# Two pads and two rounded tiles that move every float32r operand by 32 bytes or more in SBUF

## The chip, the cores and the metric

One core of one Trainium2 chip. The metric is the device time of one execution of the program in microseconds. The program before takes 1569.77 us, the median of three runs (1568.62 to 1572.6).

## The reference, cut to what is computed

Five layers work on 256 tokens of width 1024, and a context of 256 tokens beside them: first two layers that act on x alone (even: sliding-window attention and a state-space mixer; odd: attention over the 64 best keys by an index), then a joint attention layer, in which x attends to itself and to the context, a gated feed-forward layer for each of the two, a state-space layer with a convolution and chunked decays over both, and a last feed-forward layer and norm for x. Nearly all the arithmetic is dense products with weights from DRAM:

```python
z = hn @ w_in                          # 1024 x 2304, 1024 x 3144, later 1536 and 6208 columns
h = h + concat([att, ssm]) @ w_out
out = (silu(a @ w_gate) * (a @ w_up)) @ w_down      # 1024 x 2816 and back, for x twice, for the context once
```

All values are float32, and the result must be close to a float32 product.

## The kernel before, in words

A product of activations and weights is made of three products in float32r, a format of four bytes that TensorE takes at one column a cycle and that keeps fewer bits than float32. Weights and activations are each split into a high part h and a low part l = value - h; what is added up in PSUM is h x h, h x l and l x h.

Weights pass through `Weights`: `fetch` brings a chunk of 128 x 1024 float32 (512 KB) into a tile raw, on SyncE's DMA queue; `load` lets ScalarE round it into a tile h (line 178) and VectorE (or GpSimd) subtract into a tile l (line 179). `wx` holds three raw, two h and two l for x, `wc` two of each for the context, and both stand in pools on the right side of SBUF. Activations stand on the left, in pairs such as nhx and nlx (normalized x, 8 blocks of 128 x 256), fh and fl (the feed-forward's hidden values) or ysH and ysL.

Two helpers use a chunk. `feat_tiles` takes 128 weight columns as the stationary operand and streams 256 tokens past them: 8 blocks times 3 products, 24 products of 256 columns. `tok_step` takes 128 tokens as the stationary operand and streams weight columns: 2 blocks, 2 halves of tokens and 3 products, 12 products of 512 columns, or 24 of 256 columns where the chunk is cut for 256. All go through `mm` (line 129). Every product comes with its own load of 128 stationary columns (LDWEIGHTS, on the engine row PEld), which runs beside the product before it. In the state-space layer's convolution (`project`) the three channel blocks are made for x and for the context with one chunk: 24 more products for each of 3 blocks in 8 groups.

Products in plain float32 are the state-space and attention ones (`pv`, `py`, `pada`, `poff`); transposes are products with ident or flip, slices of the tile misc, as the moving operand. A few masks are added as bf16 products.

SBUF is handed out in stacks, each tile a multiple of 32 bytes in its partition. On the left lie 1,024 bytes for DMA descriptors and 128 bytes of built-in constants, then the pool con, whose first tile is misc (548 float32 values, 2,192 bytes, rounded up to 2,208), then res, act, wk and the pools of the layers. So misc starts at byte 1,152, a multiple of 64, and the tiles behind it at 32 past one. On the right the stack of wx begins 32 bytes under the end of SBUF, and its tiles start at 32 past a multiple of 64 too, as those of wc and cx below it do. Within a tile the slices go in steps of 256, 512 or 1,024 bytes. Small tiles of 32 bytes stand in some pools (sink in evat, hb in ev).

The order on each engine is made by a planner with a model of the engines' times; the pools with `reuse_waits="tile"` make it wait where two tiles share bytes.

Of the kernel before, what the change touches and what calls it, by code (L numbers as in the profile page):

```python
# [8 lines left out]
F32 = mybir.dt.float32  # L9
# [79 lines left out]
def build(tc, A):  # L89
    nc = tc.nc  # L90
    T, V, S, G, SY = nc.tensor, nc.vector, nc.scalar, nc.gpsimd, nc.sync
    es = ExitStack()
    PS = bass.MemoryType.PSUM

    def D(name):
        return A[name]

    def dram(a, off, ap):
        return bass.AP(tensor=a.tensor, offset=a.offset + off, ap=ap)

    def pool(name, bufs=1, space=None, right=False):
        kw = {"side": "right"} if right else {}
        if space is not None:
            kw["space"] = space
        else:
            kw["reuse_waits"] = "tile"
        return tc.tile_pool(name=name, bufs=bufs, **kw)

    con = es.enter_context(pool("con"))
    res = es.enter_context(pool("res"))  # L110
    act = es.enter_context(pool("act"))
    wk = es.enter_context(pool("wk", 2))
# [72 lines left out]
        return [(lambda t: t, dram(a, k0 * 128 * ncols + n0, [[ncols, 128], [128 * ncols, kt], [1, 128]]))]  # L185

    cst = ExitStack()
    wx = Weights("x", *WX, SY, es)
    wc = Weights("c", *WC, SY, cst)
    cx = cst.enter_context(pool("cx", right=True))  # L190
# [230 lines left out]
    def even_layer(hook):  # L421
        with ExitStack() as st:
            p = st.enter_context(pool("ev"))
# [11 lines left out]
            at = st.enter_context(pool("evat"))  # L435
# [10 lines left out]
            pr = s0.tile([32, 128], F32, name="ar_rows")  # L446
# [134 lines left out]
            sl = ssm.enter_context(pool("ssl"))  # L581
            yH = act.tile([128, 8, 256], F32R, tag="hx", name="yH")
            yL = act.tile([128, 8, 256], F32R, tag="lx", name="yL")
            sink = at.tile([128, 8], F32, name="sink")
            SY.dma_start(sink, dram(D("ev_sinks"), 0, [[0, 128], [1, 8]]))

            def attention(m):
# [100 lines left out]
            for q in range(4):  # L688
                split(glH[:, q], glL[:, q], uT[:, q])
            glu_w = D("ev_glu_w")  # L690
            hb = p.tile([128, 4], F32, name="hb")
            V.tensor_scalar(hb, glu_b[:, 4:8], 0.5, None, op0=ALU.mult)
            for c in range(4):
                pg = psx.tile([128, 2, 256], F32, tag="d", name="pglu")
# [803 lines left out]
    def low(f, by):  # L1498
# [6 lines left out]
        (ctx_start, ctx_qkv, ctx_attend, ctx_ffn, ctx_mod1, ctx_steps), LOW))  # L1505
    hooks = {0: [c_start], 1: [c_qkv, c_attend]}
    sc_b = even_layer(lambda i: [f() for f in hooks[i]])
    odd_layer(sc_b)
    c_ffn()
# [33 lines left out]
```

## Time and profile before

| what | us |
|---|---|
| median of 3 runs | 1569.77 |
| lowest and highest | 1568.62, 1572.6 |
| the profiled execution, its time | 1569.01 |
| the profiled execution, its span | 1567.2 |
| TensorE busy in it | 1479.1 |
| VectorE busy | 1110.6 |
| ScalarE busy | 771.3 |
| GpSimd busy | 304.2 |

The span goes from the first to the last instruction of the profiled execution; its time is a little longer. A busy TensorE is one that has a product in its pipe: products overlap, so a busy time near the span says that something is always in flight, and not how fast it goes. The pace is read from the starts of products that follow each other.

### The profile page before, as it was taken

What the parts mean: (1) busy time and instruction counts of PE and PEld (TensorE: products, weight loads), DVE (VectorE), ACT (ScalarE), POOL (GpSimd) and SP (SyncE); (2) the same over time, 40 slices, a digit from 0 to 9 for tenths busy, and PEclk for the clock granted to TensorE, in tenths of its full rate; (3) what the DMA queues carried; (4) which work ended last, traced back from release to release, by engine and by line L of the source; (5) the groups of instructions that cost most, each with busy time, mean ns of one, the idle gap of its engine ahead of it and who ended that gap; (6) DMA issues with size and microseconds to landing.
All of it is one profiled execution on the core that took longest, in us unless ns stands there. A gap on an engine that the chain in (4) does not pass through costs nothing. (4 is left out here: it accounts for less than half of the span.)

```text
span 1567.2 us, 26910 instructions
## 1 busy us (share of the span) xinstructions
PE 1479.1 (94%) x10532; PEld 1263.1 (81%) x10532; DVE 1110.6 (71%) x1825; ACT 771.3 (49%) x1386; POOL 304.2 (19%) x247
## 2 busy tenths in 40 slices
PE   6799998999999999999989999889899999799998
PEld 5574555786898888687779999888789998699997
DVE  6779996667766778666556665478988876665665
ACT  4433446654545455576444444445455544454444
POOL 2415660000100100000000000238966400200000
PEclk9899999999999999999999999898999999999999
DMA  8784565566665767633666465454534433455664
GB/s 252 237 224 143 185 172 164 142 190 211 192 187 169 219 204 201 224 109 101 199 209 190 161 186 181 126 135 123 128 106 129 109 97 121 156 164 187 194 188 135
DMA packets 306174, 264.56 MB, mean 169 GB/s; under 512 B 27441, under 2 KB 260703, under 8 KB 306048
## 3 DMA queue, kind: packets, MB, share of 16 engines
q1 hardware_dynamic: 306048, 262.85, 56.2%
q8 instruction: 83, 1.36, 0.4%
q14 instruction: 43, 0.35, 0.1%
HBM read 261.47 MB, written 1.34 MB: 168 GB/s over the span
## 5 line engine op out<-in xcount | busy, mean ns | idle before, releaser
L179 DVE TENSOR_TENSOR l<-raw,h 128x1024 fp32r<-128x1024 f32 (+2 forms) x366 | 453.4, 1241 | 268.0 <-ACT h L178 237.6
L178 ACT ACTIVATE h<-raw 128x1024 fp32r<-128x1024 f32 (+2 forms) x374 | 389.0, 1042 | 411.2 <-PE pdx L129 103.9
L129 PE MATMUL pffnx<-nhx,h 128*128 128x256 f32 x704 | 170.4, 282 | 0.0
L129 PE MATMUL pffnx<-nlx,h 128*128 128x256 f32 x704 | 170.1, 282 | 0.2 <-DVE nlx L349 0.2
L129 PEld LDWEIGHTS pffnx<-nhx,h 128*128 128x128 f32 x704 | 134.3, 191 | 1.6 <-issue 1.6
L129 PEld LDWEIGHTS pffnx<-nlx,h 128*128 128x128 f32 x704 | 133.9, 190 | 1.5 <-issue 0.8
L307 POOL TENSOR_TENSOR sums<-sums,nhalf 128x1 f32<-128x1 f32 x20 | 13.0, 652 | 536.3 <-DVE sums L303 523.4
L129 PE MATMUL pffnx<-nhx,l 128*128 128x256 f32 x704 | 96.8, 280 | 0.0
L129 PE MATMUL pffnc<-nhc,h 128*128 128x256 f32 x352 | 88.9, 287 | 0.4 <-ACT nhc L348 0.4
L129 PEld LDWEIGHTS pffnx<-nhx,l 128*128 128x128 f32 x704 | 88.4, 189 | 0.4 <-issue 0.4
L129 PE MATMUL pffnc<-nlc,h 128*128 128x256 f32 x352 | 87.9, 285 | 0.1
L179 POOL TENSOR_TENSOR l<-raw,h 128x1024 fp32r<-128x1024 f32 (+1 forms) x8 | 18.5, 2312 | 353.8 <-PE pdx L129 200.5
L129 PE MATMUL pdx<-h,nhx 128*128 128x256 f32 (+1 forms) x256 | 84.8, 347 | 1.4 <-DVE cv L1284 1.3
L129 PE MATMUL pdx<-h,nlx 128*128 128x256 f32 (+1 forms) x256 | 83.0, 341 | 0.0
L894 PE MATMUL pada<-araw,cT 128*32 128x256 f32 x704 | 72.7, 401 | 10.7 <-DMA araw<-ada_w 9.8
L129 PE MATMUL pcvx<-nhx,h 128*128 128x256 f32 x256 | 73.8, 298 | 3.8 <-DVE cv L1284 3.8
L129 PE MATMUL pdx<-h,fh 128*128 128x256 f32 (+1 forms) x264 | 77.2, 318 | 0.0
L129 PE MATMUL pdx<-h,fl 128*128 128x256 f32 (+1 forms) x264 | 77.1, 317 | 0.0
L129 PE MATMUL pcvx<-nlx,h 128*128 128x256 f32 x256 | 71.8, 290 | 0.0
L129 PEld LDWEIGHTS pffnc<-nhc,h 128*128 128x128 f32 x352 | 66.5, 189 | 2.9 <-ACT nhc L348 1.0
L129 PEld LDWEIGHTS pffnc<-nlc,h 128*128 128x128 f32 x352 | 66.6, 189 | 2.1 <-DVE nlc L349 0.5
L129 PE MATMUL pdx<-l,nhx 128*128 128x256 f32 (+1 forms) x256 | 58.5, 344 | 1.4 <-DVE l L179 1.3
(620 smaller groups left out, 3875.9 us busy)
## 6 DMA issues: line engine op xcount, KB each, us to landing
araw<-ada_w SPq DMA_DIRECT2D x88, 512.0 KB
raw<-ffn_w_gate SPq DMA_DIRECT2D x66, 512.0 KB
raw<-ffn_w_up SPq DMA_DIRECT2D x66, 512.0 KB
raw<-ffn_w_down SPq DMA_DIRECT2D x54, 512.0 KB
raw<-ssm_w_in SPq DMA_DIRECT2D x48, 512.0 KB
raw<-od_w_in SPq DMA_DIRECT2D x25, 512.0 KB
raw<-attn_w_qkv SPq DMA_DIRECT2D x24, 512.0 KB
raw<-attn_w_o SPq DMA_DIRECT2D x32, 256.0 KB
```

The source lines that it names most:

```text
L129: i = T.matmul(out, l, r, start=start, stop=stop)
L178: S.activation(h[:, :n], raw[:, :n], AF.Copy)
L179: (G if self.on_pool > 0 else V).tensor_tensor(l[:, :n], raw[:, :n], h[:, :n].bitcast(F32), op=ALU.subtract)
L307: G.tensor_tensor(s[:, 3:4], s[:, j - 1:j], nhalf[:, 0:1], op=ALU.pow)
L894: T.matmul(pt[32 * q:32 * q + 32, 0:256], cT[:, k, :], raw[:, q * 256:(q + 1) * 256], start=k == 0, stop=k == 7, tile_position=(0, 32 * q))
```

## The change

A tile of 32 bytes is put ahead of misc in con, which nothing reads or writes, and another in a pool of its own at the right end of SBUF, ahead of wx. So everything in con and in the left pools moves up by 32 bytes, and the weight pools on the right move down by 32. The tiles sink and hb are allocated with 64 bytes in place of 32, and used as before through a slice, so that the tiles behind them (Tt, and glH and glL in its place) lie at a multiple of 64 too. misc itself moves from 1,152 to 1,184. No instruction is added, removed or given another shape.

```diff
--- before.py
+++ after.py
@@ -107,6 +107,7 @@
         return tc.tile_pool(name=name, bufs=bufs, **kw)
 
     con = es.enter_context(pool("con"))
+    con.tile([128, 8], F32, name="pad")
     res = es.enter_context(pool("res"))
     act = es.enter_context(pool("act"))
     wk = es.enter_context(pool("wk", 2))
@@ -185,6 +186,7 @@
         return [(lambda t: t, dram(a, k0 * 128 * ncols + n0, [[ncols, 128], [128 * ncols, kt], [1, 128]]))]
 
     cst = ExitStack()
+    es.enter_context(pool("pr", right=True)).tile([128, 8], F32, name="padr")
     wx = Weights("x", *WX, SY, es)
     wc = Weights("c", *WC, SY, cst)
     cx = cst.enter_context(pool("cx", right=True))
@@ -581,7 +583,7 @@
             sl = ssm.enter_context(pool("ssl"))
             yH = act.tile([128, 8, 256], F32R, tag="hx", name="yH")
             yL = act.tile([128, 8, 256], F32R, tag="lx", name="yL")
-            sink = at.tile([128, 8], F32, name="sink")
+            sink = at.tile([128, 16], F32, name="sink")[:, 0:8]
             SY.dma_start(sink, dram(D("ev_sinks"), 0, [[0, 128], [1, 8]]))
 
             def attention(m):
@@ -688,7 +690,7 @@
             for q in range(4):
                 split(glH[:, q], glL[:, q], uT[:, q])
             glu_w = D("ev_glu_w")
-            hb = p.tile([128, 4], F32, name="hb")
+            hb = p.tile([128, 16], F32, name="hb")[:, 0:4]
             V.tensor_scalar(hb, glu_b[:, 4:8], 0.5, None, op0=ALU.mult)
             for c in range(4):
                 pg = psx.tile([128, 2, 256], F32, tag="d", name="pglu")
```

## Rows read from the trace of the kernel before

**Rows 1.** Page: span, TensorE's busy time and instructions, ScalarE's weight chunks.

```profile
span 1567.2 us, 26910 instructions
PE 1479.1 (94%) x10532; PEld 1263.1 (81%) x10532; DVE 1110.6 (71%) x1825; ACT 771.3 (49%) x1386; POOL 304.2 (19%) x247
...
L178 ACT ACTIVATE h<-raw 128x1024 fp32r<-128x1024 f32 (+2 forms) x374 | 389.0, 1042 | 411.2 <-PE pdx L129 103.9
```

**Rows 2.** Chain that ended last, two pieces (start us, us, what, count).

```profile
1375.12 61.22 PE pffnx L129 x527
...
1466.41 62.19 PE pffnx L129 x528
```

**Rows 3.** Windows: length, PE, PEld, DVE, ACT, POOL busy (count), clock, DMA, GB/s.

```profile
1378.10:1436.10 58.00, 58.00 (x514) 58.00 (x514) 36.61 (x51) 28.63 (x42) 0.00 (x0) 1.00 0.64 191
1436.20:1451.30 15.10, 15.10 (x69) 12.39 (x68) 7.70 (x9) 6.10 (x9) 0.00 (x0) 1.00 0.53 181
1466.20:1528.40 62.20, 62.20 (x530) 62.20 (x530) 38.99 (x55) 29.64 (x43) 0.00 (x0) 1.00 0.64 189
1528.40:1543.80 15.40, 15.40 (x68) 12.52 (x67) 7.69 (x9) 6.07 (x9) 0.00 (x0) 1.00 0.53 179
```

**Rows 4.** Same view, a stretch at the low clock, and its timeline of PE.

```profile
1008.28:1011.46 3.18, 3.18 (x16) 3.18 (x16) 2.10 (x4) 1.52 (x4) 0.00 (x0) 0.50 0.00 0
...
1009.00 0.42 PE L129 MATMUL pcvx<-nlx,h 128*128 128x256 f32 x1
...
1011.35 0.41 PE L129 MATMUL pcvx<-nlx,h 128*128 128x256 f32 x1
```

**Rows 5.** Timeline of PE (start us, us, what): a bf16 product and the next.

```profile
440.90 0.27 PE L129 MATMUL plo<-sel,flip_b 128*128 128x256 bf16 x1
441.01 0.60 PE L129 MATMUL plo<-KTo,QTo 128*128 128x256 f32 x2
```

**Rows 6.** Timeline of PE: two plain float32 products, with one between them.

```profile
121.05 0.38 PE L129 MATMUL py<-m,CT 128*32 128x256 f32 x1
...
121.48 0.38 PE L129 MATMUL py<-m,CT 128*32 128x256 f32 x1
```

**Rows 7.** Windows of line 178 alone: ScalarE's copies, one for each weight chunk.

```profile
0.00:300.00 300.00, 45.39 (x43) 0.95 0.64 191
300.00:790.00 490.00, 136.71 (x132) 1.00 0.60 182
790.00:995.00 205.00, 68.29 (x66) 0.98 0.60 186
995.00:1162.00 167.00, 25.86 (x25) 0.93 0.47 123
1162.00:1370.00 208.00, 44.42 (x43) 0.98 0.40 119
1370.00:1567.00 197.00, 68.34 (x66) 0.98 0.57 175
```

**Rows 8.** Windows of all engines by stage: PE, PEld, DVE, ACT, POOL, clock, DMA.

```profile
0.00:300.00 300.00, 264.21 (x1600) 174.27 (x1601) 233.49 (x408) 139.34 (x310) 109.25 (x99) 0.95 0.64 191
300.00:790.00 490.00, 485.95 (x3472) 405.14 (x3471) 335.04 (x587) 265.37 (x472) 17.18 (x21) 1.00 0.60 182
790.00:995.00 205.00, 200.30 (x1576) 187.55 (x1576) 131.81 (x207) 95.05 (x145) 2.14 (x4) 0.98 0.60 186
995.00:1162.00 167.00, 143.03 (x1059) 134.32 (x1058) 128.10 (x184) 80.18 (x138) 116.71 (x78) 0.93 0.47 123
1162.00:1370.00 208.00, 197.48 (x1368) 180.47 (x1368) 158.85 (x264) 101.71 (x190) 57.59 (x44) 0.98 0.40 119
1370.00:1567.00 197.00, 188.12 (x1466) 181.39 (x1466) 123.31 (x179) 89.67 (x132) 1.37 (x2) 0.98 0.57 175
```

**Rows 9.** Groups by line: transposes by ident (L1111) and by flip (L841).

```profile
L1111 PE MATMUL ptcx<-misc,P 128*128 128x128 f32 x128 | 20.1, 277 | 0.0
...
L841 PE MATMUL ppt<-misc,Tt 128*128 128x128 f32 x24 | 4.4, 279 | 0.0
```

## The prediction

> **What bounds the kernel now.** Read first the page's busy times. TensorE (PE) is busy for 1479.1 us of the 1567.2 us span [rows 1]. Busy PE is not PE at its peak, so the second view is the chain of work that ended last: its last pieces are long unbroken runs of float32r products, 527 and 528 in a row in the last feed-forward stage, with no wait between them [rows 2]. There the time is count times pace, so the third view is the pace of such a run: a stretch of the windows view divided by the products that start in it. One should take some 106.7 ns for 256 columns at the granted 2.4 GHz (PEclk 1.00). In the first half of that stage 512 products take 58.0 us, 113.3 ns each; in the second half 528 take 62.2 us, 117.8 ns each; products of 512 columns take 15.1 us for 66 (228.8 ns) and 15.4 us for 66 (233.3 ns) [rows 3]; a row counts up to three neighbours that reach over its edge. So every float32r product is 6 to 10% slower than its columns, and nothing it waits for explains that.
>
> Three rows narrow down where the loss comes from. At the lower clock it is gone: 11 products from 1009.00 to 1011.35 us take 213.6 ns each, which is 256 columns at 1.2 GHz [rows 4]. A bf16 product of 256 columns hands over after 0.11 us [rows 5], and a plain float32 one, which streams each column twice, after 0.215 us, which is 512 columns at 2.4 GHz [rows 6]; the operands of both lie at 32 bytes past a multiple of 64, as the float32r ones do now. So the loss shows only where four bytes per column are wanted at every cycle of the full clock: it is in the supply from SBUF, not in the array or in the issue.
>
> The size fits straddling. A 256-column operand is 1 KB. Starting at 32 past a multiple of 64 it touches 17 blocks of 64 bytes where an aligned one touches 16; a block is 16 columns, 17 blocks are 272 cycles, and 272 cycles at 2.4 GHz are 113.3 ns, the faster pace to the last digit [rows 3]. It doesn't fit everything: 512 columns would touch 33 blocks, 220 ns, and the rows say 228.8 and more; and the same operands at the same addresses run at 113.3 and at 117.8 ns in the two halves, so at least 4.4 ns depend on something else.
>
> **The change, part by part.** No instruction is added or removed. Four allocations grow. Today the constants begin with misc (2192 bytes, rounded up to 2208), so everything behind it on the left lies 32 past a multiple of 64; the tiles of wx and wc on the right do too. After it, all 8212 float32r products have both operands at a multiple of 64. The trace of before has no float32r product that does, so the worth is bounded, not read.
>
> Number: the 374 weight chunks [rows 1] each serve 24 products of 256 columns, or 12 of 512 (two units each); the context's share in the convolution adds 8 x 3 x 8 x 3 = 576. Together 374 x 24 + 576 = 9552 units. Pace now: the mean of 113.3, 117.8, 228.8/2 and 233.3/2 [rows 3] is 115.6 ns. Pace after, best end: 109 ns, what a stream without loss shows (0.11 us in [rows 5], half of 0.215 us in [rows 6]). Worst end: 117.8 ns, the slower pace everywhere. I take the best end, because the loss has the size of one block per product and vanishes in each row where a 17th block would be hidden. Saving: 9552 x 6.6 ns = 63 us of PE work, 0.158 us a chunk.
>
> How much of that reaches the end is read stage by stage, from the chunks per stage [rows 7] and the other engines there [rows 8]. The shares are my estimates from those rows:
> - 0 to 300 us: 43 chunks, 6.8 us. DVE is busy 233 of 300 us, POOL 109, and the state-space scan orders the work: a third, 2.3.
> - 300 to 790: 132 chunks, 20.9 us; PE busy 486 of 490: 85%, 17.7. The rest is in attention, where PE waits its turn behind DVE and ACT.
> - 790 to 995: 66 chunks, 10.4 us; PE 200 of 205: 95%, 9.9.
> - 995 to 1162: 25 chunks, 4.0 us; POOL 117 of 167 us, PE only 143: 40%, 1.6.
> - 1162 to 1370: 43 chunks and the 576 products (in part before), 10.6 us; PE 197 of 208, but groups wait for decays and gates: 70%, 7.4.
> - 1370 to 1567: 66 chunks, 10.4 us; nothing but PE: 95%, 9.9.
>
> The sum is 48.8 us. What is late next: the weight chunk's split on DVE and its copy on ACT (DVE 123 of 197 us in the last stage) and the DMAs (0.57 of the 16 engines) both have room for a pace 6% faster [rows 8]. The profiled execution took 1569.0 us, 0.8 under the median of 1569.8 and 1.8 over its span, so 1569 - 49 = 1520 us.
>
> Ident and flip move too: misc goes from a multiple of 64 to 32 past one, flip from 16 past to 48 past. Transposes by ident take 277 ns, by flip 279 [rows 9], so the start of that operand costs at most 2 ns on the program's 541 transposes by ident, 1 us, and I take nothing. Weight loads from DRAM land 32 bytes further down, DVE and ACT read and write there: no row has the other alignment; DMA has 43% of its engines free in the last stage and DVE 37%, so either sign is covered there, and I allow 3 us both ways elsewhere. The larger sink and hb push the tiles behind them by 32 to 64 bytes, and where pools of different times share space a wait can appear or go: 0 to 3 us, taken as nothing.
>
> [...]
>
> **The rivals.** A, *alignment is nothing to the stream*: the extra sixteenth is the rate at which SBUF feeds four-byte columns, wherever they start. For it: the loss doubles with the columns, as a rate would, and a block counted per product would not; and the two paces at one address. Against it: only that 113.3 ns is 272 cycles to the digit. It gives 1570 us.
> B, *half of it*: straddling is the part that varies, and all settles at 113.3 ns, or a like part goes. 9552 x 2.3 ns = 22 us, times the same survival (49/63), 17 us: 1552 us.
> C, *slower*: today moving and stationary operand start 64 bytes apart within 128 bytes (activations 32, weights 96); the left moves up by 32 and the right down by 32, so afterwards both start at 64. If the weight load and the stream, which run side by side (PEld busy 181 of 197 us in the last stage [rows 8]), get in each other's way when they start in the same half, the slower pace holds everywhere: 9552 x 2.2 ns x 0.78 = 16 us, 1586 us. It decides against the change when more than the share of products now at 117.8 goes there and nothing is won on the straddle. The two paces at equal addresses say that such a meeting of streams exists.
> D, *it doesn't do what it says*: a consumer is left at 32. Tile sizes are multiples of 32, and those ahead of float32r tiles that are odd multiples come in pairs, but for the ones that the diff changes; so small, and like A in time.
>
> **How the numbers follow.** Forecast 0.45 (1520 us, own range 1503 to 1536: all 63 us survive, or half), B 0.17, A with D 0.22, C 0.16. What a measurement of this kernel can tell from no change is about 0.3%, 5 us. B lies beyond that bound, so faster is 0.62; A and a little of C give 0.23 for the same; slower is 0.15. The range goes from 1503 to 1582: it takes in the forecast's own range, B and A, and the smaller half of C.
>
> **What would show it.** In the last stage, the 512 and 528 products without a wait: right at 109 to 110 ns, B at 113, A at both paces as now, C at 118 throughout; products of 512 columns at 216, 227, 229 to 233, or 233 and more. The weight load's pace follows. The stages before 300 and from 995 to 1162 us should shrink least. Transposes by ident at 277 ns, as before. It would be wrong if the paces don't move (the step "the loss has the size of a block" falls), or if they do and the span doesn't: then the survival shares are wrong, and the wait that took the place is to be found on DVE's l, ACT's h or raw's DMA.

## The result and the profile after

The changed kernel takes 1585.78 us, the median of four runs (1581.62 to 1587.9); the kernel before, on the same chip, takes 1569.19 (1567.05 to 1572.6). The ratio is 1.010, its 95% interval 1.0073 to 1.0128: slower by one per cent. The forecast was 1520 us and its range ended at 1582; rival C, which had it slower, gave 1586.

First the page of after: the span, the engines, and the group of ScalarE's weight copies that answers to the one in [rows 1].

```profile
span 1584.2 us, 26910 instructions
PE 1502.0 (95%) x10532; PEld 1286.8 (81%) x10532; DVE 1111.9 (70%) x1825; ACT 772.0 (49%) x1386; POOL 302.5 (19%) x247
...
L179 ACT ACTIVATE h<-raw 128x1024 fp32r<-128x1024 f32 (+2 forms) x374 | 388.6, 1041 | 426.1 <-PE pdx L130 106.2
```

The instruction counts are those of before, and so is the order on every engine. TensorE is busy 22.9 us longer. A copy of a weight chunk takes 1041 ns (1042 before), all of VectorE 1111.9 us (1110.6): the other engines did not notice their new addresses. Transposes by ident and flip, the groups of [rows 9], didn't either:

```profile
L1113 PE MATMUL ptcx<-misc,P 128*128 128x128 f32 x128 | 20.0, 277 | 0.0
...
L843 PE MATMUL ppt<-misc,Tt 128*128 128x128 f32 x24 | 4.5, 279 | 0.0
```

So the time went into the pace of the products. The windows of the last feed-forward stage, as in [rows 3] (length, PE, PEld, DVE, ACT, POOL busy with counts, clock, DMA share, GB/s):

```profile
1390.10:1451.40 61.30, 61.30 (x514) 61.30 (x513) 36.60 (x51) 28.74 (x42) 0.00 (x0) 1.00 0.61 182
1451.40:1466.40 15.00, 15.00 (x69) 12.40 (x68) 7.67 (x9) 6.07 (x9) 0.00 (x0) 1.00 0.52 181
1466.50:1545.60 79.10, 79.10 (x662) 79.10 (x661) 50.30 (x71) 35.39 (x49) 0.00 (x0) 1.00 0.63 185
1545.60:1560.60 15.00, 15.00 (x69) 12.41 (x68) 7.70 (x9) 6.07 (x9) 0.00 (x0) 1.00 0.56 183
```

Each count holds three neighbours from over the edge. 511 products of 256 columns in 61.30 us are 120.0 ns each, and 659 in 79.10 us again 120.0; before it was 113.3 in the first half and 117.8 in the second. Products of 512 columns take 15.00 us for 66, 227.3 ns, in both halves; before 228.8 and 233.3. So the two kinds moved in opposite directions. A cycle here is an estimate, the time of one column at the full clock: 256 columns took 213.6 ns at a granted clock of 0.50 [rows 4], so 106.8 at 1.00, 2.4 columns a ns; and m1 below has 106.7 ns between products of 256 and 512 columns (120.0 and 226.7). In such cycles 120.0 ns are 288, 32 more than the columns; the 512-wide ones, taken from the starts of a long run, need 545, 33 more. For these two widths the loss no longer grows with the columns: it is 32 cycles or so for each product.

The growth by stage, in windows whose bounds lie at the same products as those of [rows 8]:

```profile
0.00:305.03 305.03, 269.07 (x1600) 177.98 (x1601) 234.02 (x408) 139.49 (x310) 108.24 (x99) 0.95 0.63 188
305.03:798.66 493.63, 490.90 (x3472) 410.59 (x3471) 335.55 (x587) 265.93 (x472) 17.24 (x21) 1.00 0.60 181
798.66:1006.14 207.48, 203.56 (x1576) 191.20 (x1576) 131.82 (x207) 94.96 (x145) 2.05 (x3) 0.98 0.61 184
1006.14:1173.45 167.31, 145.47 (x1058) 136.85 (x1058) 126.24 (x184) 80.31 (x138) 116.01 (x78) 0.93 0.46 122
1173.45:1381.80 208.35, 199.73 (x1368) 183.36 (x1368) 160.91 (x264) 101.60 (x189) 57.62 (x44) 0.98 0.40 119
1381.80:1584.00 202.20, 193.23 (x1466) 186.78 (x1466) 123.34 (x179) 89.66 (x132) 1.37 (x2) 0.97 0.56 170
```

The stages are 5.0, 3.6, 2.5, 0.3, 0.4 and 5.2 us longer, together 17.0. Since the order is the same, each product has its twin in the other trace. Summed over those that nothing holds up in either trace, the pace of 256-wide products cost 1.1, 5.5, 3.8, 2.6, 3.2 and 5.7 us in the six stages, 22.0 in all, and that of 512-wide ones gave back 1.5. So 20.5 us of pace became 17.0 us of span.

### The profile page after: what moved, and what is told of

It reads as the page before. It is cut to its first block, busy times and chain, and to the rows that moved or that the text cites. A ratio compares the mean times of both kernels' runs of the same rounds, so it can differ in the third digit from the quotient of the medians.

```text
span 1584.2 us, 26910 instructions
## 1 busy us (share of the span) xinstructions
PE 1502.0 (95%) x10532; PEld 1286.8 (81%) x10532; DVE 1111.9 (70%) x1825; ACT 772.0 (49%) x1386; POOL 302.5 (19%) x247
## 5 line engine op out<-in xcount | busy, mean ns | idle before, releaser
L179 ACT ACTIVATE h<-raw 128x1024 fp32r<-128x1024 f32 (+2 forms) x374 | 388.6, 1041 | 426.1 <-PE pdx L130 106.2
L130 PE MATMUL pffnx<-nhx,h 128*128 128x256 f32 x704 | 174.7, 285 | 0.0
L130 PE MATMUL pffnx<-nlx,h 128*128 128x256 f32 x704 | 174.4, 285 | 0.3 <-DVE nlx L351 0.2
```

The source lines that it names most:

```text
L130: i = T.matmul(out, l, r, start=start, stop=stop)
L179: S.activation(h[:, :n], raw[:, :n], AF.Copy)
```

## What was to be told apart

Call distance the start of a product's weights less the start of its moving operand, in bytes. Modulo 128 it is 64 before (32 and 96) and 0 after (64 and 64), but for some 500 of the 8,212 products, which kept 64; m1 shows that modulo 256 is the right measure. Theory 1: the load of the next weights and the stream get in each other's way, and the distance alone sets the pace; where the operands lie matters to nothing. Theory 2: the pace comes from the absolute starts, so that a start at a multiple of 64 is what costs. The bench kernels m1 to m3 below are trains of products on one pair of tiles, with x as filling: they compute nothing of the reference, and serve for the pace alone.

## m1: one pair of tiles, the starts varied

```diff
+ mo = m0 // 4 + (i % 7) * n
+ wo = w0 // 4 + (i // 2 % 8) * 128
+ T.matmul(pt[0:w, 0:n], wt[:, wo:wo + w], mv[:, mo:mo + n], start=i == 0, stop=i == count - 1)
```

> A bench of its own: 38 runs of 96 float32r products (48 of 512 columns) without a wait between them, which compute nothing of the reference; only the byte at which the streamed operand starts (m) and the distance d to the start of the weights are varied. Theory 1 (the stream of one product and the weight load of the next meet in SBUF; only the distance between them counts): at d = 0 a product of 256 columns takes 120 ns, at d = 64 it takes 113 or 118 ns, the same for m = 0, 32, 64 and 96; the loss comes from the weight load, so with 512 columns it stays at some 14 ns (227 ns), with 64 weight columns it is half (113 ns) and with 32 a quarter (110 ns). Theory 2 (the start itself counts): 120 ns for m = 0 and 64 whatever d is, 113 or 118 ns for m = 32 and 96. Theory 3 (neither; the pace comes from how a run happens to begin): paces between 113 and 120 ns without an order in d or m, and the repeats of d = 64 and d = 0 at the end differ among themselves.

The timeline of PE (start, length, tile, count); the pace of a group is the time from its start to the next group's start, divided by its count. Groups pad to paf have the moving operand at 0 and the weights at 48, 64 and 80; pai and paj have the weights at 128 and 160; par and pas have the two at 32 and 96, and at 64 and 64; paw to pay are 512-wide at distances 0, 32, 64, and pbb at 192; pbi to pbl alternate 64, 0, 64, 0.

```profile
46.12 11.47 PE L45 MATMUL pad<-mv,wt 128*128 128x256 f32 x96
57.43 11.05 PE L45 MATMUL pae<-mv,wt 128*128 128x256 f32 x96
68.31 11.57 PE L45 MATMUL paf<-mv,wt 128*128 128x256 f32 x96
...
102.62 11.55 PE L45 MATMUL pai<-mv,wt 128*128 128x256 f32 x96
114.01 11.68 PE L45 MATMUL paj<-mv,wt 128*128 128x256 f32 x96
...
204.76 11.47 PE L45 MATMUL par<-mv,wt 128*128 128x256 f32 x96
216.07 11.67 PE L45 MATMUL pas<-mv,wt 128*128 128x256 f32 x96
227.58 11.47 PE L45 MATMUL pat<-mv,wt 128*128 128x256 f32 x96
...
261.70 11.09 PE L45 MATMUL paw<-mv,wt 128*128 128x512 f32 x48
272.63 11.35 PE L45 MATMUL pax<-mv,wt 128*128 128x512 f32 x48
283.82 11.36 PE L45 MATMUL pay<-mv,wt 128*128 128x512 f32 x48
295.02 11.40 PE L45 MATMUL paz<-mv,wt 128*128 128x512 f32 x48
...
317.42 11.16 PE L45 MATMUL pbb<-mv,wt 128*128 128x512 f32 x48
328.41 11.06 PE L45 MATMUL pbc<-mv,wt 128*128 128x512 f32 x48
...
394.04 11.04 PE L45 MATMUL pbi<-mv,wt 128*128 128x256 f32 x96
404.92 11.68 PE L45 MATMUL pbj<-mv,wt 128*128 128x256 f32 x96
416.44 11.47 PE L45 MATMUL pbk<-mv,wt 128*128 128x256 f32 x96
427.75 11.68 PE L45 MATMUL pbl<-mv,wt 128*128 128x256 f32 x96
```

pae, at distance 64, takes 10.88 us for 96, 113.3 ns; pad and paf beside it take 117.8 and 118.8. pas, both operands at 64, takes 11.51 us, 119.9; par, both at the starts of the kernel before, 117.8. Over the last 48 products of each group, distance 0 gave 120.0 ns with the moving operand at 0, 32, 64 and 96 alike, and distance 64 gave 113.3 or 117.8. The other distances under 128 gave 118.3 at 16 and 32, 117.8 at 48, 118.8 at 80, 118.6 at 96 and 120.0 at 112. 512-wide it is the other way round: 226.7 ns at distance 0 in the second half of its group (227.7 over the whole) and 233.3 at 32 and 64. All paces of both kernels appear here, with no other engine at work. Theory 2 falls. Theory 1 holds in its main point: the distance decides which paces occur, and the place of the operands doesn't. That the distance alone sets the pace does not hold, since the repeats of 64 differ among themselves, as theory 3 had it.

Modulo 128 turned out to be too coarse. At 128 the pace is 118.6 ns (pai) where 0 and 256 have 120.0, at 160 it is 120.0 where 32 has 118.3, and 512-wide it is 229.0 at 192 (pbb) where 64 and 320 have 233.3. At 256 and 384 the 256-wide paces are those of 0 and 128 again. So the distance counts modulo 256. Taken so, the kernel before has mainly two: 64 where activations stream past weights, and 192 where activations are the weights. Its 512-wide runs in [rows 3] stand at 192, and m3, further down, saw both of their paces there: about 229 ns behind most trains, 233.3 behind two.

Two things did not fit. pbi and pbk have the same addresses, and run at 113.3 and 117.8: the one comes after products with 32 weight columns, the other after products at distance 0. So the two paces of [rows 3] are no matter of stage or neighbours; a train keeps what it begins with. And with only 64 or 32 weight columns the pace was 113.3 at distance 0 as at 64 (pbe to pbh): a loss of 16 cycles stays, though the weight columns shrink to a quarter; theory 1 had 110 for 32 columns.

## e1 and e2: distance against alignment in the kernel

e1 is the kernel before with 64 bytes ahead of misc: nothing lies at a multiple of 64, and the distance is 0. e2 is the changed kernel with 64 more: everything lies at a multiple of 64, and the distance is 64 modulo 128 (modulo 256, the 64 and the 192 of the kernel before have changed places).

```diff
 # e1, against before
+    con.tile([128, 16], F32, name="pad")
 # e2, against after
-    con.tile([128, 8], F32, name="pad")
+    con.tile([128, 24], F32, name="pad")
```

> The kernel before with 64 bytes ahead of the constants and nothing else: everything stays 32 past a multiple of 64, but the left side's operands now start at 96 within 128 bytes, as the weights on the right do (distance 0). Theory 1 (the distance counts): 120 ns for 256 columns, 227 ns for 512, and 1586 us, like the changed kernel, though nothing is aligned to 64. Theory 2 (the alignment counts): 113 and 118 ns as before, 1570 us.

> The changed kernel with a pad of 96 bytes in place of 32 ahead of the constants: all operands at a multiple of 64 as in the changed kernel, but the left ones at 0 and the weights on the right at 64 within 128 bytes (distance 64, as in the kernel before). Theory 1 (the distance counts): 113 and 118 ns as before, 1570 us. Theory 2 (the alignment counts): 120 ns and 1586 us.

e1 took 1586.3 us (ratio 1.0096, 1.0074 to 1.0118), as the changed kernel; e2 took 1572.05 (1.0006, 0.9995 to 1.0018), as the kernel before. The windows of the last stage, e1 first: two runs of 256-wide products and one of 512-wide.

```profile
1391.00:1452.00 61.00, 61.00 (x510) 61.00 (x509) 36.63 (x51) 28.33 (x42) 0.00 (x0) 1.00 0.61 180
1467.10:1546.20 79.10, 79.10 (x662) 79.10 (x661) 50.24 (x71) 35.40 (x49) 0.00 (x0) 1.00 0.64 186
1452.00:1467.00 15.00, 15.00 (x69) 12.40 (x68) 7.67 (x9) 6.07 (x9) 0.00 (x0) 1.00 0.54 180
```

Then e2, the same three:

```profile
1380.70:1441.10 60.40, 60.40 (x514) 60.40 (x514) 36.63 (x51) 28.59 (x42) 0.00 (x0) 1.00 0.61 184
1456.80:1531.50 74.70, 74.70 (x662) 74.70 (x661) 50.15 (x71) 35.34 (x49) 0.00 (x0) 1.00 0.68 197
1441.30:1456.70 15.40, 15.40 (x69) 12.40 (x68) 7.76 (x9) 6.09 (x9) 0.00 (x0) 1.00 0.56 178
```

e1 runs at 120.0 ns (659 in 79.10 us) and 227.3 (66 in 15.00). e2 has both paces of before, with the halves exchanged: 117.7 in the first (513 in 60.40 us), 113.4 in the second (659 in 74.70), and 233.3 for 512 columns. Alignment to 64 bytes buys nothing and costs nothing that these runs resolve (e2's interval ends at 0.18%, some 3 us); the distance accounts for the 16 us. The changed kernel's own trace says it too: 237 products of 256 columns that kept distance 64 in it, on tiles that moved together, average 116.9 ns, against 119.75 for the 6,027 at distance 0.

The 113.3 and 120.0 ns of m1 (pbi and pbj), at distances that differ by the weights' address alone, say that the address of the load changes the stream's pace. By what path it does so, no run shows.

## e3 and e4: half of the change

Only the left pad, or only the right one: the distance becomes 32 either way, with other absolute starts.

```diff
 # e3, against before
+    con.tile([128, 8], F32, name="pad")
 # e4, against before
+    es.enter_context(pool("pr", right=True)).tile([128, 8], F32, name="padr")
```

> The change's first edit alone: 32 bytes ahead of the constants, nothing on the right, no tile rounded up. The left operands lie at a multiple of 64, the weights on the right stay 32 past one; the distance in the products with streamed activations goes from 64 to 32. Theory 1 (distance, priced by the first bench: 118.3 ns at 32 against 113.3 or 117.8 at 64): about half to three quarters of the change's loss, 1576 to 1584 us. Theory 2 (alignment of the left side): the whole loss in the products that stream activations.

> The change's second edit alone: 32 bytes at the right end, nothing on the left, no tile rounded up. The weights lie at a multiple of 64, the activations don't; the distance is 32 as with the left pad alone. Theory 1 (distance): the same as the left pad alone, 1576 to 1584 us. Theory 2 (alignment): another time than the left pad alone, as different operands are aligned.

e3 took 1580.04 us (1.0073, 1.005 to 1.0096), e4 1580.48 (1.007, 1.0043 to 1.0097). One window of each, first e3:

```profile
1387.40:1447.90 60.50, 60.50 (x513) 60.50 (x511) 36.59 (x51) 28.49 (x42) 0.00 (x0) 1.00 0.61 183
```

and e4:

```profile
1387.00:1447.50 60.50, 60.50 (x513) 60.50 (x513) 36.60 (x51) 28.61 (x42) 0.00 (x0) 1.00 0.61 184
```

511 products in 60.50 us are 118.4 ns in both; over all products of the kind the means are 118.32 and 118.31, the bench's 118.33 at distance 32. Two layouts with different absolute starts and one distance are the same kernel in time.

## m2: how the loss depends on width, and what makes the two paces

The same bench with 128 to 512 columns on 32 or 128 weight columns; then distances 48 to 80 in steps of 4, each after a group at distance 0; then narrow products (32 weight columns) ahead of trains. One such sequence (columns, weight columns, the two starts, count):

```diff
+ ("s", 256, 128, 0, 0, 96), ("s", 256, 32, 0, 64, 1), ("s", 256, 128, 0, 64, 96)
```

> A second bench in the manner of the first, computing nothing of the reference: the streamed width with 32 and 128 weight columns, fine steps of the distance d, and what stands ahead of a run. Theory 1a (the loss has two parts: a sixteenth of the columns which the stream loses by itself, and the meeting with the weight load): with 32 weight columns the pace is N x 17/16 at 2.4 GHz for every width N (128: 56.7, 192: 85, 384: 170, 512: 227 ns), and at d = 0 with 128 weight columns 16 cycles more at 256 columns. Theory 1b (a fixed 16 cycles each product): N + 16 cycles (128: 60, 512: 220 ns). Of the two paces at d = 64: theory S (the pace is set by how the run begins and then holds) expects 117.8 ns behind a run at d = 0 and 113.3 ns behind a run with 32 weight columns, and that one product with 32 weight columns in between is enough to turn it; theory R (it is random) expects no such order.

With 32 weight columns, products of 128 columns took some 144 cycles, 16 over, as 1b had it (60 ns, an estimate: 56 of them took 3.70 us from 13.00 us on, the eight before 107.5 ns each, and seven more at that pace leave 60 ns for the rest). Those of 192, 256, 320, 384, 448 and 512 columns took 88.4, 113.5, 143.3, 173.3, 202.2 and 231.6 ns, or 212, 272, 344, 416, 485 and 556 cycles: 20, 16, 24, 32, 37 and 44 over their columns. That is neither a sixteenth of the columns nor a fixed 16, so both readings of the rest (1a and 1b) fall, and what it is stays open. With 128 weight columns at distance 0 it was 32 over at 256, 320, 384 and 512 columns, but 76 at 192 (111.4 ns) and 48 at 448 (206.4 ns). At distance 64 products of 192, 320 and 384 columns took just as long as at 0 (111.4, 146.9 and 173.3 ns), and those of 448 took 37 over (202.3 ns). So the distance counts at 256, 448 and 512 columns and not at the three other widths; and at 384 columns 32 weight columns are no quicker than 128. The meeting of load and stream is thus no general price of distance 0, and what makes it depend on the width is open.

The entry is clearer. Timeline of PE: pay at distance 64 after a group at 0; and pbp at 0, one narrow product, pbr at 64.

```profile
260.18 11.47 PE L54 MATMUL pay<-mv,wt 128*128 128x256 f32 x96
271.49 11.68 PE L54 MATMUL paz<-mv,wt 128*128 128x256 f32 x96
...
449.63 11.68 PE L54 MATMUL pbp<-mv,wt 128*128 128x256 f32 x96
461.15 0.28 PE L54 MATMUL pbq<-mv,wt 128*32 128x256 f32 x1
461.27 11.04 PE L54 MATMUL pbr<-mv,wt 128*128 128x256 f32 x96
472.15 11.68 PE L54 MATMUL pbs<-mv,wt 128*128 128x256 f32 x96
```

pay takes 11.31 us, 117.8 ns a product. One product with 32 weight columns ahead of it, and the same train (pbr) takes 10.88 us, 113.3, as theory S had it. In the three benches together 64 ran at 117.8 in all six trains behind distance 0, and at 113.3 in all six behind narrow products; at 320, which is 64 modulo 256, the one train behind distance 0 (m1's pan) ran at 113.5. Among the distances from 48 to 80 only 52 and 76 ran at 113.3 behind a group at distance 0.

## m3: the entry at more distances

Each distance is entered three times: after distance 0, after 512-wide products at 192, and after four narrow products.

```diff
+ ("s", 256, 128, 0, 0, 48), ("s", 256, 128, 0, d, 72), ("s", 512, 128, 0, 192, 24),
+ ("s", 256, 128, 0, d, 72), ("s", 256, 32, 0, d, 4), ("s", 256, 128, 0, d, 72)
```

> A third bench in the same manner, computing nothing of the reference: each distance d is entered behind a run at d = 0, behind products of 512 columns, and behind four products with 32 weight columns. In the second bench d = 52 and 76 went to 113.3 ns behind a run at d = 0, where 64 went to 117.8. Theory S1 (the fast pace of 113.3 ns exists at most distances, and how a run begins decides; 52 and 76 have the better entry): 113.3 ns in all three entries at 52 and 76, 117.8 then 113.3 behind the narrow products at 64 and 192. Theory S2 (luck of that entry): 52 and 76 come out at 113.3 in some of the entries only.

The timeline of PE for distance 52 (pai, pak and pam are the trains, paj the 512-wide entry, pal the narrow one):

```profile
60.49 8.37 PE L51 MATMUL pai<-mv,wt 128*128 128x256 f32 x72
68.70 5.66 PE L51 MATMUL paj<-mv,wt 128*128 128x512 f32 x24
74.19 8.80 PE L51 MATMUL pak<-mv,wt 128*128 128x256 f32 x72
82.83 0.63 PE L51 MATMUL pal<-mv,wt 128*32 128x256 f32 x4
83.30 8.33 PE L51 MATMUL pam<-mv,wt 128*128 128x256 f32 x72
```

At 52 the train runs at 114.0, 120.0 and 113.3 ns (8.21, 8.64 and 8.16 us for 72) by what came ahead of it. At 64 the three are 117.8, 117.8 and 113.3; at 204 they are 123.1, 113.3 and 113.3. Only 76 and 192 gave 113.3 from all three. At 44, 60, 68, 84, 180 and 212 no entry changed the pace, which was between 117.2 and 120.0. So S1 is right for 76 and S2 for 52, and neither as a whole: 113.3 appeared at only five of the fourteen distances. 120.0 isn't the worst pace there is, and 113.3 remains the best.

## e5 and e6: entries and 512-wide products in the kernel

e5 puts twelve narrow products ahead of the feed-forward's and other long trains; each writes a part of PSUM that the train then starts anew. e6 adds 192 bytes ahead of ysH, so that the 192 products of 512 columns of the state-space output go from distance 64 to 0.

```diff
 # e5, against before (in feat_tiles; tok_step likewise)
+        if lead:
+            mm(uses[0][1][0:32], wh[:, 0, 0:32], uses[0][0](0)[0], True, True, mark)
 # e6, against e5
+            p.tile([128, 48], F32, name="pady")
```

> The kernel before, with 12 products of 256 columns and 32 weight columns put ahead of long runs (each half of x's two feed-forward layers, their way back where it turns to 256 columns, and the odd layer's gates); their results are overwritten by the next product, so the output is the same. Theory S (the entry sets the pace until something interrupts): the runs behind them take 113.3 ns; some 2,000 of the products that now take 117.8 ns are behind one, 2,000 x 4.4 ns = 9 us less 12 x 0.11 us, 1561 to 1566 us. Theory R (random, or fixed by the distance): both paces as before, 1570 to 1572 us.

> The same with 192 bytes ahead of ysH and ysL, which serve 192 products of 512 columns as weights: their distance to the streamed operand goes from 64 to 0 (within 256 bytes). Theory 1 (the distance counts, and with 512 columns 0 is the best, 226.7 against 233.3 ns in the benches): these products take 226.7 ns in place of 231 to 236 and the time is 192 x 6.7 ns = 1.3 us under the kernel with the lead products alone. Against: 512 columns take 231 to 236 ns wherever ysH starts.

e5 took 1584.56 us (1.0101, 1.0081 to 1.0121), well outside what was expected. Two windows of its last stage, both behind a lead:

```profile
1392.70:1450.90 58.20, 58.20 (x515) 58.20 (x515) 36.62 (x51) 28.63 (x42) 0.00 (x0) 1.00 0.64 191
1466.30:1544.00 77.70, 77.70 (x662) 77.69 (x661) 50.14 (x71) 35.19 (x49) 0.00 (x0) 1.00 0.65 189
```

The first runs at 113.4 ns (513), the second at 117.7 (660): in the kernel one narrow product ahead of a train did not always settle its pace. Once it did: in the odd layer's gates the 72 products ahead of the lead at 441.82 us take 8.48 us, 117.8 ns each, and the 70 behind it 7.94 us, 113.4 each, at the same distance. And the planner, given twelve more products, put all engines into another order from TensorE's 290th product on; the last stage begins at 1392.7 us instead of 1378.1, with the paces of before in it. So e5 shows that the leads did not steer reliably, and not what steering would be worth.

e6 took 1582.98 us (1.0084, 1.0059 to 1.0108), 1.6 under e5, with intervals that overlap. The 512-wide run it was made for:

```profile
1361.50:1375.60 14.10, 14.10 (x63) 11.65 (x62) 8.94 (x11) 7.49 (x12) 2.04 (x1) 1.00 0.65 201
```

62 products in 14.10 us are 227.4 ns, where the same run in e5 and in the kernel before has 233.5. The pace followed the distance as in the bench. Over all 192 the mean goes from 233.3 to 228.4, so they could save 192 x 5 ns, about 1 us, and that is less than these runs resolve.

## e7 and e8: the two distances that the bench liked

Both start the activations elsewhere in a widened tile, so that 256-wide products stand at distance 76 (e7) or 192 (e8, modulo 256; 64 modulo 128), and keep the pad of e6 ahead of ysH. The order on the engines is that of before.

```diff
+    def act_tile(tag, name):
+        return act.tile([128, 2112], F32R, tag=tag, name=name)[:, 61:2109].rearrange("p (k t) -> p k t", k=8)
 # e8: [:, 32:2080]
-          H = act.tile([128, 8, 256], F32R, tag="h" + key, name="nh" + key)
+          H = act_tile("h" + key, "nh" + key)
```

> The kernel before with the activations' tiles widened by 256 bytes and used from byte 244 on, and 192 bytes ahead of ysH; no instruction and no order changes. The 5184 products that stream activations past weights go from a distance of 64 to 76, 1296 products with those activations as weights from 192 to 180, the 192 with ysH from 64 to 0. Theory S1 (at 76 a run finds the fast pace from any beginning, as in all four entries of the benches): 113.3 ns for the first kind (now 116.1 in the mean), 118.2 and 233.3 ns for the second (now 116.3 and 231.2), 227 ns for ysH: -14.5 + 2.9 - 1.2 us of PE work, at the share of 0.78 some 10 us: 1556 to 1564 us. Theory S2 (in the kernel the beginnings are too many): the paces stay mixed, 1566 to 1575 us.

> The same with the activations used from byte 128 on: the 5184 products at a distance of 192, the 1296 at 64, ysH at 0. At 192 the benches found 113.3 ns in four entries and 117.8 in one. Theory S1: as at 76, 1556 to 1566 us, if the kernel's beginnings are like the four. Theory S2: 113.3 and 117.8 ns mixed as before, 1566 to 1575 us. If the pace at 192 is 117.8 throughout: 1575 to 1580 us.

e7 took 1584.33 us (1.0109, 1.0088 to 1.013). Two windows of its last stage:

```profile
1400.00:1454.00 54.00, 54.00 (x440) 54.00 (x439) 31.98 (x46) 24.54 (x37) 0.00 (x0) 1.00 0.59 177
1486.00:1548.00 62.00, 62.00 (x519) 62.00 (x518) 38.17 (x53) 28.32 (x43) 0.00 (x0) 1.00 0.63 187
```

Some 517 products in 62.0 us, 120 ns; in the first half of that stage it was about 123 (some 438 products in 54.0 us), and over all 4,727 at that distance the mean is 120.63. The bench's 113.3 did not carry over, and both theories missed. In the bench the streamed operand stood at 0 and the weights at 76, in e7 they stand at 20 and 96 modulo 128; whether that is what matters was not separated.

e8 took 1573.24 us (1.0042, 1.0024 to 1.006). Both halves of its last stage:

```profile
1379.60:1440.10 60.50, 60.50 (x515) 60.50 (x515) 36.64 (x51) 28.69 (x42) 0.00 (x0) 1.00 0.61 184
1471.30:1533.00 61.70, 61.70 (x527) 61.70 (x526) 38.48 (x54) 29.14 (x43) 0.00 (x0) 1.00 0.64 189
```

514 products in 60.50 us and 524 in 61.70: 117.7 ns in both. Here nearly every train took the slower of the two paces (mean 117.40 over 4,862), where the kernel before has both (mean 116.09), and the quicker ysH products didn't make up for it. The time lies in S2's range, but the paces were hardly mixed; 117.8 throughout had been given 1575 to 1580. e2 has these two distances as well, and half of its last stage ran at 113.4: the distance says which paces there are, and not which of them a train gets. No version found beats the kernel before.

## Why the prediction was wrong, step by step

- *What bounds the kernel.* Right: long trains of float32r products, whose time is count times pace. The pace moved, and the last stage, which has nothing else, moved by the full price: 5.7 less 0.5 us of pace, 5.2 us of span.
- *"The loss is in the supply from SBUF, not in the array or in the issue."* Right for the part that moved. It didn't ask which of the two supplies: with 128 weight columns the loss at 256 columns goes from 16 to 32 cycles, 113.3 to 120.0 ns, by the weights' address alone (m1), so the load of the next weights belongs to it. For the 16 cycles that stay at every distance no run shows where they arise.
- *"The size fits straddling", one block of 64 bytes per product.* This is the step that failed. That 272 cycles are 17 blocks of 16 columns was a coincidence of numbers: at distance 0 the pace is 288 cycles with the operand aligned to 64 (pas) or not, and 272 appears aligned (e2's second half) and not aligned (before). What the runs show in its place is the distance between weights and stream: with every operand aligned the 256-wide pace is 120.0 at distance 0 (the changed kernel) and 117.7 and 113.4 in e2. The two misfits that the prediction itself named, 512 columns at 228.8 ns instead of 220 and two paces at one address, were the evidence against it.
- *The pace after.* I took the best end, 109 ns, borrowed from bf16 and plain float32 [rows 5, 6]. Neither row is the pace of a product in a stream: the kernel issues 64 py products and the trace has 128 records of them, so 0.215 us is half a product, and the bf16 product at 442.53 us hands over after 0.03 us, not 0.11. At a granted clock of 1.00 no train of 48 or more float32r products of 256 columns showed a pace under 113.3, in the kernels or in the benches. The worst end, 117.8, was too good by 2.2 ns: at distance 0 it is 120.0. An end taken from the worst of two rows is not a bound on a layout that none of them has.
- *Rival C.* What it named is what happened: weights and stream that start together, and a slower pace. Its mechanism, the two getting in each other's way, is borne out for 256 columns by the narrow weights, whose products take 113.3 ns at distance 0 as at 64 (m1); it does not cover the 512-wide products, which got quicker there, nor the widths that don't care (m2). Its price was wrong: it moved all products to 117.8 ns, 2.2 ns on 9,552 units, 21 us. Measured, the 256-wide ones went from 116.1 to 119.6 ns in the mean and the 512-wide ones got quicker by 1.3; by twin products 22.0 less 1.5 us, 20.5. Two errors of price cancel, and 1586 agrees with 1585.8 in part by luck. A chance of 0.16 was too low, since the two paces at equal addresses, which I counted for it, had no other explanation in the rows.
- *Survival.* 0.78 of the pace was to reach the end; the span grew by 17.0 us on 20.5 of pace, 0.83, which looks like a hit and is luck in part. In the first stage 3.9 us of the growth are not pace; without them 13.1 of 20.5 us came through, 0.64. 790 to 995 (2.5 of 3.4 us) and 300 to 790 (3.6 of 5.2) came out under their 95% and 85%. From 995 to 1370 us, where I had 40 and 70%, 0.7 of 5.6 us survived: waits took up most of the rest, as TensorE's idle time in these two stages fell from 34.5 to 30.5 us. The first stage grew by 5.0, of which pace is 1.1. Some 2.4 us of that come in one place, where TensorE stands idle for ScalarE's PT and then runs 3.4 us at a granted clock of 0.50 (271.98 to 275.38 us), where the kernel before has 1.00 (260 to 280 us). In the timeline of PE of after:

```profile
271.41 0.66 PE L1113 MATMUL ptcc<-misc,P 128*128 128x128 f32 x4 [2.17 <-ACT PT L1118]
```

The number in brackets is the idle time before. e1 has a step of about that size at 225 to 240 us instead, so its place isn't fixed by the layout; I did not follow it further.
- *Edits taken at nothing.* Right: ident at 277 and flip at 279 ns as before, DVE and ACT with the same durations, no wait from the larger sink and hb.
- *Rivals A and B.* A's "alignment is nothing" is true as far as e2 resolves it, but its conclusion of no change isn't: the padding moved the distance. A's rate, a fixed share of the columns, falls with the widths of m2. B's uniform 113.3 never came. D falls: the float32r operands of the changed program do lie at multiples of 64.

## What to carry to other kernels

Where a train of products with a weight load each runs off its column count, look at the start of the weights less the start of the moving operand, modulo 256, before looking at either alone, and change one pool's offset at a time: 32 bytes on either side cost this kernel 0.7%, on both 1.0%. A loss that matches a block size to the digit in one row has to match the other widths too before it counts as a cause. And when one address shows two paces, a model that explains the pace by the address alone is already incomplete.

## What the runs showed of the hardware that was not expected

- The pace of a float32r product of 256 columns with 128 weight columns lay between 113.3 and 123.1 ns by the distance of weights and stream: 120.0 at 0, 113.3 or 117.8 at 64, 118.3 at 32 (m1), 113.3 or 123.1 at 204 (m3). Of 512 columns it was 226.7 at 0, 233.3 at 32 and 64 (m1), and about 229 or 233.3 at 192 (m3), so the best distance depends on the width. The distance counts modulo 256 bytes, not 128: 120.0 ns at 0 and 256, 118.6 at 128 (m1).
- At distance 0 the loss was 32 cycles for 256, 320, 384 and 512 columns alike (120.0, 146.9, 173.4 and 226.7 ns), but 76 for 192 and 48 for 448 (111.4 and 206.4 ns); at 192, 320 and 384 columns distance 64 lost as much as 0 (m1, m2).
- A train can have two stable paces at one pair of addresses (113.3 and 117.8 at 64; 114.0, which settles at 113.3, and 120.0 at 52) and keeps the one that it enters with: 96 products in the bench, 659 in e2. In the bench one product with 32 weight columns ahead of it was enough to choose (117.8 to 113.3 ns, m2); in the kernel (e5) it was at 441.82 us and not at the last stage's second half, and why is open.
- With 32 or 64 weight columns the pace at 256 columns is 113.3 ns at distances 0 and 64 alike (m1): these 16 cycles of loss have nothing to do with the distance. Their cause is open.
